# A hybrid of four chunked recurrences on one core: SSD's outputs, gates and norms with channels on partitions, heads on column tiles, norm sums by products

## The chip, the cores and the metric

The kernel runs on one core of a Trainium2 chip. The metric is the device time of one execution, in microseconds; the time before is the median of three runs.

## The reference

One layer of a decoder trunk over 2048 tokens of 1024 channels, float32. The input is normalized (`rmsnorm`) and multiplied by one matrix `w_in`, whose columns feed four mixers of 512 channels each: GLA, mLSTM, HGRN2 and Mamba-2 SSD. Each mixer is a causal recurrence in chunks; its output is normalized in groups, multiplied by a `silu` gate z, and all four go through `w_out`, a residual sum and a last `rmsnorm`. The part that the change is about:

```python
def ssd_chunked(x, a, Bm, Cm, chunk):
    ...
    a_cs = jnp.cumsum(a, axis=-1)
    L = segsum_exp(a)
    CB = jnp.einsum('bclgn,bcsgn->bgcls', Cm, Bm)
    y_diag = jnp.einsum('bgrcls,bcsgrp->bclgrp', CB[:, :, None] * L, x)
    ...
    y_off = jnp.einsum('bclgn,bcgrpn,bgrcl->bclgrp', Cm, states, jnp.exp(a_cs))
    return (y_diag + y_off).reshape(Bsz, S, H, P)

def ssd_branch(...):
    ...
    y = ssd_chunked(xs * dt[..., None], dt * A, Bm, Cm, SSD_CHUNK)
    y = (y + D[:, None] * xs).reshape(Bsz, S, D_BRANCH)
    return grouped_rmsnorm(y * jax.nn.silu(z), norm_w, SSD_GROUPS)
```

SSD has 8 heads of 64 channels in two groups (four heads each share B and C, 128 states), chunks of 128 tokens, and a norm over each group's 256 channels. HGRN2 has 4 heads with 128 keys and 128 values; its scores are `q_i k_j` weighted by a product of decays for each key channel.

## The kernel before, in words

The tokens are cut into two halves of 1024 (`TH`), eight chunks of 128 each. `run` goes through both halves, and in each through the units g0, g1 (GLA), s0, s1 (SSD, four heads each), h0, h1 (HGRN2, two heads each), m0, m1 (mLSTM); then `out_phase` multiplies by `w_out`. A mixer's result goes to the tensor `y` in HBM and is read again in `out_phase`.

The projections split float32 into two parts (high and low, fp32r) and sum three products. `proj_chan` puts 128 output channels on the partitions and 512 tokens on the columns (TensorE tile `ps_c`); `proj_tok2` and `proj_wide` put tokens on the partitions (tile `ps_t`). All other products are plain float32; each stands in the profile as two records of TensorE, as each has two weight loads; a transpose is one record. All of them go through the helper `mm`, line 124, so the profile is read by tiles. The weights come through a ring of nine slots (`load_slot`), issued on the SP queue; in the first half they are split by ScalarE and VectorE and also written to HBM for the second half.

The program is written unit by unit, but a scheduler at build time sets the order on each engine, so a unit's products stand between those of the next unit's projections. Each engine then works through its own list in order. PSUM has four slots for projections (tag `proj`) and four for all else (tag `t`).

In `ssd` (lines 871 to 948) the convolved x, B and C have channels on the partitions (`xc`, `bt`, `ct`). The z gates are projected with tokens on the partitions (`szs`). Then, for each chunk: x and B are transposed (`ps_xt`); the decays `L` of four heads are made from the loaded rows `ab`; `ps_s` holds C·B; the four heads' outputs are four products of 64 columns into `ps_o` (stationary: `L` of a head, moving: x·dt of that head), C·H is one product of 256 columns; `ps_u` is the update of the state `H`. VectorE and GpSimd put the outputs together, multiply by the gate; ScalarE squares with accumulation (`squares`), and at the end of the unit `finish` makes the norm's factors, one for each token, thus one for each partition, scales the rows and writes them through `store` (32x32 transposes on VectorE, four DMAs for each 128 channels and four chunks).

In `lin_steps` HGRN2's scores are built level by level: for block sizes b = 1, 2, 4 to 64 VectorE multiplies the decays of b neighbours into `kb` (line 521) and `qf` (line 522), and TensorE forms the scores between neighbouring blocks. For HGRN2 (`nh == 1`) `mixed` gathers the keys of an even and an odd chunk into one stationary tile of 128 (two ScalarE copies, lines 478 and 479) and makes four products of 128 columns (`ps_s`). The levels 1 to 16 are put into the score tiles by masked copies (lines 499, 545, 546), the levels 32 and 64 by ScalarE copies of the blocks that lie on the diagonal. GLA (`nh == 2`, 64 keys a head) makes its levels 32 and 64 with products of 32 and 64 stationary columns, and its state update (`ps_u<-o_v,t2k`) with two heads beside each other in the partitions of one result.

Of the kernel before, what the change touches and what calls it, by code (L numbers as in the profile page):

```python
# [10 lines left out]
F32 = mybir.dt.float32  # L11
# [4 lines left out]
AF = mybir.ActivationFunctionType  # L16
ALU = mybir.AluOpType
# [4 lines left out]
P = 128  # L22
# [57 lines left out]
def _params(i):  # L80
    cols = []

    def add(key, a):
        PC[key] = sum(c.shape[1] for c in cols)
        cols.append(np.asarray(a, np.float32))

    def rep(v):
        return np.broadcast_to(np.asarray(v).reshape(1, -1), (P, np.asarray(v).size))

    add("nw", i["norm_w"][0].reshape(KT, P).T)  # L90
    add("bw", np.concatenate([i["gla_norm_w"][0], i["ml_norm_w"][0], i["hg_norm_w"][0], i["ssd_norm_w"][0]]).reshape(16, P).T)
# [26 lines left out]
class Kernel:  # L118
# [65 lines left out]

    def row_bcast(self):

        nc = self.nc
# [269 lines left out]
    def lin_steps(self, nh, f, kb, qp, v, sz, car, eps, ycol, vt=None):  # L457
# [58 lines left out]
        while b < C:  # L516
# [18 lines left out]
            if nh == 1:  # L535
# [335 lines left out]
    def ssd(self, q):  # L871
# [12 lines left out]
        w = self.weights(("sz", q))  # L884
        szs = [self.sztile().rearrange("p c (a d) -> p (c a d)", a=1).rearrange("p (c d) -> p c d", c=4) for _ in range(2)]
# [4 lines left out]
        dD = self.dd[:, h4].unsqueeze(2).to_broadcast([P, 4, 64])  # L890
        ss = self.small.tile([P, 16], F32, tag="f_ss", name="f_ss")[:, :8]

        def finish():
            rs = self.rms(ss, 256, 256 * EPS, self.rs2)
            nc.vector.tensor_tensor(rs, rs, self.rs, op=ALU.mult)
            for g in range(2):
                self.scale_rows(szs[g], rs[:, 4 * g:4 * g + 4])
                for j in range(2):
                    self.store(szs[g][:, :, j * P:(j + 1) * P], g, 1536 + 256 * q + j * P)

        for g in range(2):
            yb = szs[g]
            for u in range(2):
                ab = self.up.tile([P, 4, 256], F32, tag="qf", name="ab")
                t0 = g * 512 + u * 256
                nc.sync.dma_start(ab, self.rows[4 + 4 * q:8 + 4 * q, t0:t0 + 256].unsqueeze(0).broadcast_to([P, 4, 256]))
                for j in range(2):
                    c = 2 * u + j
                    cc = 4 * g + c
                    cs = slice(cc * C, (cc + 1) * C)  # L910

                    def hb(t):
                        return t[:, cc, h4].unsqueeze(2).to_broadcast([P, 4, 64])

                    def v4(t):
                        return t.rearrange("p (h d) -> p h d", h=4)

                    pt = self.psp.tile([P, 512], F32, tag="t", name="ps_xt")
                    for i, src in enumerate((xc[0], xc[1], bt)):
                        nc.tensor.transpose(pt[:, i * P:(i + 1) * P], src[:, cs], self.ident)  # L920
                    xx, tb = self.t2k(), self.t2k()
                    xdt, xdd, y1, bk = xx[:, :256], xx[:, 256:], tb[:, :256], tb[:, 256:384]
                    nc.vector.tensor_tensor(v4(xdt), v4(pt[:, :256]), hb(self.dt), op=ALU.mult)
                    nc.vector.tensor_tensor(v4(y1), v4(pt[:, :256]), dD, op=ALU.mult)
                    nc.scalar.copy(bk, pt[:, 256:384])
                    nc.vector.tensor_tensor(v4(xdd), v4(pt[:, :256]), hb(self.dec), op=ALU.mult)
                    ps = self.psp.tile([P, C], F32, tag="t", name="ps_s")
                    self.mm(ps, bt[:, cs], ct[:, cs])
                    L = self.t2k().rearrange("p (h t) -> p h t", h=4)
                    for h in range(4):  # L930
                        nc.vector.scalar_tensor_tensor(out=L[:, h], in0=ab[:, h, j * C:(j + 1) * C], scalar=self.acs[:, cc, 4 * q + h:4 * q + h + 1], in1=self.cmask, op0=ALU.subtract, op1=ALU.min)
                    nc.scalar.activation(L, L, AF.Exp)
                    nc.vector.tensor_tensor(L, L, ps[:, None].to_broadcast([P, 4, C]), op=ALU.mult)
                    po = self.psp.tile([P, 512], F32, tag="t", name="ps_o")
                    for h in range(4):
                        self.mm(po[:, h * 64:(h + 1) * 64], L[:, h], xdt[:, h * 64:(h + 1) * 64])
                    self.mm(po[:, 256:512], ct[:, cs], H)
                    pu = self.psp.tile([P, 256], F32, tag="t", name="ps_u")
                    self.mm(pu, bk, xdd)
                    nc.vector.tensor_tensor(y1, y1, po[:, 0:256], op=ALU.add)  # L940
                    t1 = self.t2k()[:, :256]
                    nc.vector.tensor_tensor(v4(t1), v4(po[:, 256:512]), hb(self.eacs), op=ALU.mult)
                    nc.gpsimd.tensor_tensor(y1, y1, t1, op=ALU.add)
                    nc.gpsimd.tensor_tensor(yb[:, c], y1, yb[:, c], op=ALU.mult)
                    nc.vector.tensor_tensor(v4(H), v4(H), self.el[:, h4, cc:cc + 1].to_broadcast([P, 4, 64]), op=ALU.mult)
                    nc.vector.tensor_tensor(H, H, pu, op=ALU.add)
            self.squares(yb, ss[:, 4 * g:4 * g + 4])
        finish()


    def flat(self, tag, n, dtype=F32):
# [153 lines left out]
    def prepare(self, cp):  # L1105
# [90 lines left out]
```

## Time and profile before

| what | value |
|---|---|
| median of three runs | 2130.73 us (2127.08 to 2130.87) |
| profiled execution: its own time | 2130.25 us |
| its span, first to last instruction | 2128.4 us |
| TensorE busy (matmul) | 2075.1 us, 97% |
| VectorE busy | 1212.8 us, 57% |
| ScalarE busy | 759.0 us, 36% |
| GpSimd busy | 61.0 us, 3% |
| mean granted TensorE clock | 0.993 |

The difference between an execution's own time and its span, 1.85 us, lies around the instructions. A busy time of TensorE is the union of modelled durations of products that overlap in the pipe; the pace of a stream of products is read from how many stand in a stretch of the chain, or from the starts in the timeline. PE is TensorE, DVE VectorE, ACT ScalarE, POOL GpSimd, SP the queue that issues most DMAs.

### The profile page before, as it was taken

What the parts mean: (1) busy time and instruction counts of PE and PEld (TensorE: products, weight loads), DVE (VectorE), ACT (ScalarE), POOL (GpSimd) and SP (SyncE); (2) the same over time, 40 slices, a digit from 0 to 9 for tenths busy, and PEclk for the clock granted to TensorE, in tenths of its full rate; (3) what the DMA queues carried; (4) which work ended last, traced back from release to release, by engine and by line L of the source; (5) the groups of instructions that cost most, each with busy time, mean ns of one, the idle gap of its engine ahead of it and who ended that gap; (6) DMA issues with size and microseconds to landing.
All of it is one profiled execution on the core that took longest, in us unless ns stands there. A gap on an engine that the chain in (4) does not pass through costs nothing.

```text
span 2128.4 us, 31817 instructions
## 1 busy us (share of the span) xinstructions
PE 2075.1 (97%) x12094; PEld 1767.2 (83%) x12094; DVE 1212.8 (57%) x2962; ACT 759.0 (36%) x1889; POOL 61.0 (3%) x96
## 2 busy tenths in 40 slices
PE   7999999999999999999999999999999999999998
PEld 6877898887888888997879887888889898888887
DVE  4465769676565673725466858482826276533332
ACT  5622333435344445324222324342433245212111
POOL 0000001100000000000000201000000000000000
PEclk9999999999999999999999999999999999999999
DMA  8524344535152546342124342322324126422221
GB/s 284 200 90 128 102 139 144 154 91 166 35 189 80 188 117 225 114 160 73 39 98 124 91 118 60 128 55 90 111 89 110 62 103 214 147 89 96 98 74 50
DMA packets 228809, 251.24 MB, mean 118 GB/s; under 512 B 144808, under 2 KB 160280, under 8 KB 228656
## 3 DMA queue, kind: packets, MB, share of 16 engines
q1 hardware_dynamic: 222176, 229.81, 34.3%
q10 hardware_dynamic: 6480, 19.40, 2.6%
q8 instruction: 95, 1.56, 0.3%
q14 instruction: 58, 0.48, 0.1%
HBM read 160.70 MB, written 88.45 MB: 117 GB/s over the span
## 4 chain that ended last, share of the span: by engine, by line
PE 77%; DVE 10%; DMA 6%; ACT 5%; issue 2%; POOL 0%; SPq 0%; DVEq 0%; ACTq 0%; POOLq 0%
PE ps_t L124 24%; PE ps_c L124 21%; PE ps_out L124 15%; PE ps_o L124 5%; PE ps_s L124 5%; DMA raw<-w 2%; PE ps_u L124 2%; PE ps_g L124 2%; DMA ab<-rows 1%; DVE w L223 1%; ACT t2k L637 1%; DVE kc L766 1%; DVE kb L521 1%; DMA t2k<-xT 1%; DMA o_v<-w_out 1%
## 5 line engine op out<-in xcount | busy, mean ns | idle before, releaser
L124 PE MATMUL ps_t<-w,uh 128*128 128x512 f32 (+1 forms) x2560 | 635.7, 339 | 0.5 <-DMA w<-wk 0.5
L124 PE MATMUL ps_c<-uh,w 128*128 128x512 f32 x1792 | 579.8, 400 | 7.2 <-ACT uh L156 7.2
L124 PEld LDWEIGHTS ps_t<-w,uh 128*128 128x128 f32 x2560 | 440.9, 190 | 51.7 <-DMA w<-wk 0.7
L124 PE MATMUL ps_t<-w,ul 128*128 128x256 f32 (+1 forms) x1280 | 432.8, 339 | 0.0
L124 PEld LDWEIGHTS ps_c<-uh,w 128*128 128x128 f32 x1792 | 338.7, 191 | 76.1 <-ACT uh L156 7.6
L124 PE MATMUL ps_c<-ul,w 128*128 128x512 f32 x896 | 357.5, 399 | 0.3 <-DVE ul L157 0.3
L124 PEld LDWEIGHTS ps_t<-w,ul 128*128 128x128 f32 x1280 | 243.7, 190 | 24.1
L124 PEld LDWEIGHTS ps_c<-ul,w 128*128 128x128 f32 x896 | 171.1, 191 | 34.8 <-DVE ul L157 1.1
L223 DVE TENSOR_TENSOR w<-raw,w 128x512 fp32r<-128x512 f32 (+2 forms) x125 | 82.6, 671 | 84.6 <-ACT w L222 83.9
L222 ACT CAST w<-raw 128x512 fp32r<-128x512 f32 (+2 forms) x125 | 74.1, 604 | 82.6 <-DMA raw<-w 51.7
L124 PE MATMUL ps_out<-woh,o_qp 128*128 128x512 f32 x288 | 92.6, 390 | 0.0
L1002 DVE TENSOR_TENSOR o_sz<-o_sz,ps_out 128x512 f32<-128x512 f32 (+1 forms) x33 | 22.0, 670 | 123.6 <-PE ps_out L124 122.3
L124 PE MATMUL ps_out<-woh,o_v 128*128 128x512 f32 (+1 forms) x213 | 75.4, 389 | 0.0
L1003 ACT ACTIVATE ST<-o_sz 128x512 f32<-128x512 f32 (+1 forms) x33 | 20.4, 618 | 123.1 <-DVE o_sz L1002 123.1
L124 PEld LDWEIGHTS ps_out<-woh,o_qp 128*128 128x128 f32 x288 | 54.1, 188 | 11.5
L307 ACT ACTIVATE sz<-ps_t,ss 128x128 f32<-128x128 f32 (+1 forms) x96 | 33.7, 399 | 74.0 <-PE ps_t L124 62.9
L124 PE MATMUL ps_g<-w,uh 128*128 128x288 f32 x256 | 52.9, 302 | 5.9 <-ACT w L222 2.9
L124 PE MATMUL ps_out<-wol,o_qp 128*128 128x512 f32 x144 | 56.2, 391 | 0.3 <-DVE wol L963 0.3
L762 DVE TENSOR_TENSOR craw<-ps_c,rb 128x512 f32<-128x512 f32 x64 | 43.7, 684 | 21.6 <-PE ps_c L124 21.6
L786 ACT ACTIVATE v<-ps_t,ss 128x128 f32<-128x128 f32 x64 | 23.5, 368 | 86.8 <-PE ps_t L124 86.8
L637 ACT ACTIVATE t2k<-ps_o 128x128 f32<-128x128 f32 x128 | 34.6, 286 | 53.6 <-PE ps_o L124 52.6
L521 DVE TENSOR_TENSOR kb<-kb,pl 128x512 f32<-128x512 f32 x72 | 49.9, 693 | 6.3 <-PE ps_s L124 6.3
(355 smaller groups left out, 3357.3 us busy)
## 6 DMA issues: line engine op xcount, KB each, us to landing
wk<-w SPq DMA_DIRECT2D x116, 512.0 KB, 4.4
w<-wk SPq DMA_DIRECT2D x116, 512.0 KB, 5.3
raw<-w SPq DMA_DIRECT2D x115, 256.0 KB, 3.3
y<-t2k SPq DMA_DIRECT2D x256, 64.0 KB, 2.0
t2k<-y SPq DMA_DIRECT2D x64, 256.0 KB, 3.2
t2k<-xT SPq DMA_DIRECT2D x32, 256.0 KB, 4.3
ab<-rows SPq DMA_DIRECT2D x16, 512.0 KB, 5.1
o_sz<-x ACTq DMA_DIRECT2D x16, 512.0 KB, 3.3
```

The lines of the kernel that those rows point to most:

```text
L124: self.nc.tensor.matmul(out, l, r, start=start, stop=stop, skip_group_check=shared)
L222: nc.scalar.copy(t[:, 0, cs], raw[:, cs])
L223: nc.vector.tensor_tensor(t[:, 1, cs], raw[:, cs], t[:, 0, cs].bitcast(F32), op=ALU.subtract)
L307: nc.scalar.activation(out[:, j], ps[:, j], AF.Tanh, scale=self.rsh[:, t + j:t + j + 1])
L521: nc.vector.tensor_tensor(kv[:, :, 0], kv[:, :, 0], pv[:, :, 1:2].to_broadcast([P, n, b]), op=ALU.mult)
L637: self.nc.scalar.activation(junk, ob[:, c], AF.Square, accum_out=ss[:, c:c + 1])
L762: nc.vector.tensor_tensor(rw, ps, self.rb[:, b * 512:(b + 1) * 512], op=ALU.mult)
L766: nc.vector.scalar_tensor_tensor(out=acc, in0=raw[:, k:k + TH], scalar=cw[k], in1=acc, op0=ALU.mult, op1=ALU.add)
L786: nc.scalar.activation(self.mv[i][:, t, :P], ps[:, i * P:(i + 1) * P], AF.Identity, scale=self.rs[:, t:t + 1])
L1002: nc.vector.tensor_tensor(xt[:, ns], xt[:, ns], ps, op=ALU.add)
L1003: nc.scalar.activation(junk[:, ns], xt[:, ns], AF.Square, accum_out=ss[:, i:i + 1])
```

## The change

1. The z gates of SSD are projected with channels on the partitions (`proj_chan`), four results of 512 tokens for each unit and half; the row factors `rb` are multiplied in by VectorE, and the gate is formed by tanh.
2. SSD's outputs are formed with channels on the partitions: for each head one product of the state `H` (64 stationary columns) with `ce` = C·exp(a), and one of x·dt (64 stationary columns) with `L`; two heads lie in partitions 0 to 63 and 64 to 127 of one result. D·x, the sum and the gate take two VectorE instructions for 128 channels and two chunks. GpSimd's part goes away.
3. The norm's sums over 256 channels are products: the squares (ScalarE) stationary, a column of ones moving, one column of result (`ps_q`).
4. The factors go to all partitions by the new function `bcast`, made from `row_bcast`: a transpose, a ScalarE copy, a write to HBM, a broadcast read. Then `zg` is multiplied and written to `y` in one DMA for each 128 channels.
5. HGRN2's levels 32 and 64 are products of 32 and 64 stationary columns, on four and two column tiles; the odd chunks' keys are still taken in reverse (`kr`, one ScalarE copy).

```diff
+    def bcast(self, col, out, tag):
         nc = self.nc
         pt = self.psp.tile([P, 512], F32, tag="t", name="ps_rb")
-        nc.tensor.transpose(pt[:NC, :P], self.rs, self.ident)
+        nc.tensor.transpose(pt[:NC, :P], col, self.ident)
         row = self.t2k()[:NC, :P]
         nc.scalar.copy(row, pt[:NC, :P])
...
+        nc.sync.dma_start(out, rows.broadcast_to([P, TH]))
...
-                ps = mixed(b, qf.rearrange("p (c n two b) -> p c n two b", c=NC, two=2, b=b)[:, :, :, 1])
+                kr = self.t2k()[:, :256].rearrange("p (c n b) -> p c n b", c=NC // 2, b=b)
+                nc.scalar.copy(kr, flipped(C - 1 - b, 2 * b, 64 // b, b))
+                ps = self.psp.tile([P, NC // 2, 2, 64 // b, b], F32, tag="t", name="ps_s")
+                for c in range(NC // 2):
+                    for n in range(64 // b):
+                        for t in range(2):
+                            k0 = (2 * c + t) * C + 2 * n * b
+                            p0 = C - (2 * n + 1) * b if t else 2 * n * b
+                            kk = kr[:, c, 64 // b - 1 - n] if t else kb[:, k0:k0 + b]
+                            self.mm(ps[p0:p0 + b, c, t, n], kk, qf[:, k0 + b:k0 + 2 * b])
...
-        for u, ps in self.proj_tok2(w):
-            self.silu2(szs[u // 2][:, 2 * (u % 2):2 * (u % 2) + 2], ps, 2 * u)
+        for j in range(2):
+            for b in range(2):
+                bs = slice(b * 512, (b + 1) * 512)
+                ps = self.proj_chan(("sz", q), j, b)
+                nc.vector.tensor_tensor(zg[j][:, bs], ps, self.rb[:, bs], op=ALU.mult)
...
-                    for h in range(4):
-                        self.mm(po[:, h * 64:(h + 1) * 64], L[:, h], xdt[:, h * 64:(h + 1) * 64])
-                    self.mm(po[:, 256:512], ct[:, cs], H)
...
+                ce = self.t2k().rearrange("p (h t) -> p h t", h=4)
+                nc.scalar.activation(ce, ab[:, :, js], AF.Exp)
+                nc.vector.tensor_tensor(ce, ce, ct[:, None, cs].to_broadcast([P, 4, C]), op=ALU.mult)
+                for i in range(2):
+                    for l, r, start in ((H, ce, True), (xdt, L, False)):
+                        for h in (2 * i, 2 * i + 1):
+                            o = h % 2 * 64
+                            self.mm(po[o:o + 64, i, j], l[:, h * 64:(h + 1) * 64], r[:, h], start=start, stop=not start)
...
-            self.squares(yb, ss[:, 4 * g:4 * g + 4])
-        finish()
+            for i in range(2):
+                nc.vector.scalar_tensor_tensor(out=xc[i][:, us], in0=xc[i][:, us], scalar=self.dd[:, 2 * q + i:2 * q + i + 1], in1=po[:, i], op0=ALU.mult, op1=ALU.add)
+                nc.vector.tensor_tensor(zg[i][:, us], zg[i][:, us], xc[i][:, us], op=ALU.mult)
+                nc.scalar.activation(sq[:, i], zg[i][:, us], AF.Square)
+            pq = self.psp.tile([P, 2], F32, tag="t", name="ps_q")
+            for j in range(2):
+                for i in range(2):
+                    self.mm(pq[:, j:j + 1], sq[:, i, j * C:(j + 1) * C], self.tri[:, P - 1:P], start=i == 0, stop=i == 1)
+            nc.scalar.copy(ss[:, 2 * u:2 * u + 2], pq)
+        nc.vector.tensor_scalar(out=ss, in0=ss, scalar1=1.0 / 256, scalar2=256 * EPS, op0=ALU.mult, op1=ALU.add)
+        rn = self.flat("v", TH)
+        self.bcast(self.rsqrt(ss, 8), rn, "nsd")
+        for i in range(2):
+            nc.vector.tensor_tensor(zg[i], zg[i], rn, op=ALU.mult)
...
+            nc.sync.dma_start(self.y[t0:t0 + NC, :, :, 12 + 2 * q + i].rearrange("c b r a s -> (b r) c (a s)"), zg[i].rearrange("p (c t) -> p c t", c=NC))
```

The scheduler then sets another order. Three places show it; line numbers are those of the respective kernel.

TensorE in a chunk of s1 in the first half, between the projection products of h0 (`ps_t`); before:

```order
L124 MATMUL ps_t<-w,uh 128x512 x2
L124 MATMUL ps_o<-t2k 128x64 x4
L124 MATMUL ps_o<-hst,ct 128x256
L124 MATMUL ps_u<-t2k 128x256
L920 MATMUL ps_xt<-cf,xc 128x128 x2
L920 MATMUL ps_xt<-cf,v 128x128
L124 MATMUL ps_s<-ct,v 128x128
```

and of the change, an odd chunk of the same unit (`ps_o<-t2k,hst` are the products of H with `ce`, `ps_o<-t2k` those of x·dt with `L`; the last row is the pair's first norm product):

```order
L124 MATMUL ps_o<-t2k,hst 64x128 x2
L124 MATMUL ps_t<-w,uh 128x512 x2
L124 MATMUL ps_o<-t2k 64x128 x2
L124 MATMUL ps_o<-t2k,hst 64x128 x2
L124 MATMUL ps_o<-t2k 64x128 x2
L124 MATMUL ps_t<-w,ul 128x512
L124 MATMUL ps_t<-w,uh 128x512 x2
L124 MATMUL ps_t<-w,ul 128x512
L124 MATMUL ps_t<-w,uh 128x512 x2
L124 MATMUL ps_t<-w,ul 128x512
L124 MATMUL ps_t<-w,uh 128x512 x2
L124 MATMUL ps_q<-cf,t2k 128x1
```

A chunk's output products were one group of five; now they are eight on column tiles, and most chunks have them in two blocks with other products between.

TensorE where s1 ends and the levels of HGRN2's first head begin, first half; before:

```order
L124 MATMUL ps_t<-w,ul 128x512
L124 MATMUL ps_s<-qp,t2k 128x128 x4
L124 MATMUL ps_s<-qp,kb 128x128 x4
L124 MATMUL ps_s<-qp,t2k 128x128 x4
L124 MATMUL ps_t<-w,uh 128x512 x2
L124 MATMUL ps_t<-w,ul 128x512
L124 MATMUL ps_t<-w,uh 128x512 x2
L124 MATMUL ps_s<-qf,t2k 128x128 x4
L124 MATMUL ps_t<-w,ul 128x512
```

and of the change (`ps_rb` is the transpose in `bcast`; the x8 are the levels b = 4 and b = 8):

```order
L124 MATMUL ps_t<-w,ul 128x512
L124 MATMUL ps_q<-cf,t2k 128x1 x4
L194 MATMUL ps_rb<-cf,rs_y 8x128
L124 MATMUL ps_s<-qp,t2k 128x128 x4
L124 MATMUL ps_s<-qp,kb 128x128 x4
L124 MATMUL ps_s<-qp,t2k 128x128 x4
L124 MATMUL ps_s<-qf,t2k 128x128 x8
L124 MATMUL ps_t<-w,uh 128x512 x2
```

The projection products that stood between the levels have moved behind b = 8. In the second half 11 of them stand between the last norm product and the transpose, and 5, 5 and 3 between the transpose and the levels.

VectorE at the same place; before:

```order
L521 TENSOR_TENSOR kb<-kb,pl 128x256x2
L546 COPY_PREDICATED ST_93<-mask,ps_s 128x4x32x2
L545 COPY_PREDICATED ST_93<-mask,ps_s 128x4x64
L521 TENSOR_TENSOR kb<-kb,pl 128x128x4
L546 COPY_PREDICATED ST_93<-mask,ps_s 128x4x32x2
L499 COPY_PREDICATED ST_93<-mask,ps_s 128x4x16x4 x2
L522 TENSOR_TENSOR qf<-qf,pl 128x128x4
```

and of the change, where `o_v` is `rn`, the tile that the broadcast read fills:

```order
L525 TENSOR_TENSOR kb<-kb,pl 128x256x2
L550 COPY_PREDICATED ST_93<-mask,ps_s 128x4x32x2
L549 COPY_PREDICATED ST_93<-mask,ps_s 128x4x64
L317 SCALAR_TENSOR_TENSOR sz<-sz,ps_t 128x128
L550 COPY_PREDICATED ST_93<-mask,ps_s 128x4x32x2
L525 TENSOR_TENSOR kb<-kb,pl 128x128x4
L966 TENSOR_TENSOR sz<-sz,o_v 128x1024 x2
L503 COPY_PREDICATED ST_93<-mask,ps_s 128x4x16x4 x2
L526 TENSOR_TENSOR qf<-qf,pl 128x128x4
```

The two instructions of line 966 have come between the level's `kb` and `qf` steps, and VectorE reaches the second only behind them; the same in the second half.

## Rows read from the trace of the kernel before

**Rows 1.** The page: busy us (share of the span) xinstructions; slices: granted clock in tenths.
```profile
PE 2075.1 (97%) x12094; PEld 1767.2 (83%) x12094; DVE 1212.8 (57%) x2962; ACT 759.0 (36%) x1889; POOL 61.0 (3%) x96
...
PEclk9999999999999999999999999999999999999999
```
**Rows 2.** Windows: the two SSD loops; length, then busy us of PE, PEld, DVE, ACT, POOL.
```profile
285.00:450.00 165.00, 163.61 (x926) 141.58 (x926) 127.98 (x317) 63.84 (x139) 24.65 (x32) 1.00 0.44 134
1160.00:1320.00 160.00, 158.93 (x896) 136.65 (x895) 117.83 (x297) 52.12 (x115) 25.56 (x32) 1.00 0.33 96
```
**Rows 3.** The chain in order of time: start us, us, what.
```profile
1224.56 23.03 PE ps_t L124 x192
...
1637.23 21.79 PE ps_c L124 x96
```
**Rows 4.** Timeline, TensorE in one SSD chunk: start us, us, engine, line, operation.
```profile
391.64 1.08 PE L124 MATMUL ps_o<-t2k 128*128 128x64 f32 x8 [0.35 <-DVE t2k L933]
...
392.55 0.65 PE L124 MATMUL ps_o<-hst,ct 128*128 128x256 f32 x2
...
393.04 0.59 PE L124 MATMUL ps_u<-t2k 128*128 128x256 f32 x2
```
**Rows 5.** Timeline, TensorE in GLA: products on column tiles and their neighbours.
```profile
224.66 1.11 PE L124 MATMUL ps_s<-qf,kb 64*32 64x32 f32 x64
...
228.19 1.15 PE L124 MATMUL ps_s<-qf,kb 64*64 64x64 f32 x32
...
231.54 0.40 PE L124 MATMUL ps_c<-ul,w 128*128 128x512 f32 x1
231.87 1.09 PE L124 MATMUL ps_u<-o_v,t2k 128*64 128x128 f32 x16
232.90 1.27 PE L124 MATMUL ps_o<-o_v,ST 128*128 128x128 f32 x9
```
**Rows 6.** Timeline, TensorE in the levels of HGRN2's first head; in brackets, idle before.
```profile
454.50 1.16 PE L124 MATMUL ps_s<-qp,t2k 128*128 128x128 f32 x8 [0.84 <-ACT t2k L479]
455.50 1.06 PE L124 MATMUL ps_s<-qp,kb 128*128 128x128 f32 x8
456.39 1.14 PE L124 MATMUL ps_s<-qp,t2k 128*128 128x128 f32 x8
...
458.96 1.16 PE L124 MATMUL ps_s<-qf,t2k 128*128 128x128 f32 x8 [0.27 <-ACT t2k L479]
```
**Rows 7.** Timeline of SP in `row_bcast`; the page's issues: count, KB, us to landing.
```profile
55.00 0.51 SPq L193 DMA_DIRECT2D rsd<-t2k  x1
59.59 0.35 SPq L195 DMA_DIRECT2D rb<-rsd  x1
...
rb<-rsd SPq DMA_DIRECT2D x2, 512.0 KB, 3.6
```
**Rows 8.** Groups by line and shape, VectorE: count, busy us, mean ns, idle before.
```profile
L522 DVE TENSOR_TENSOR qf<-qf,pl 128x512 f32<-128x512 f32 x72 | 50.4, 701 | 4.3 <-PE ps_s L124 4.0 <-ACT qp L531 0.2
L499 DVE COPY_PREDICATED ST<-mask,ps_s 128x256 f32<-128x256 uint8 x64 | 29.0, 513 | 5.2 <-PE ps_s L124 4.9
L545 DVE COPY_PREDICATED ST<-mask,ps_s 128x256 f32<-128x256 uint8 x16 | 12.1, 757 | 0.3
L140 DVE SCALAR_TENSOR_TENSOR rs_y<-rs_t,rs_y 128x8 f32<-128x8 f32 x66 | 10.8, 164 | 1.6
L466 DVE TENSOR_TENSOR qf<-qp,f 128x1024 f32<-128x1024 f32 x8 | 10.1, 1262 | 0.5 <-PE ps_o L124 0.3
```
**Rows 9.** A wait of TensorE, and the windows around it (PEclk is third from the end).
```profile
124.16 3.56 PE L124 MATMUL ps_s<-qf,kb 64*128 64x64 f32 x32 [2.23 <-DVE kb L521]
...
117.00:124.00 7.00, 4.93 (x43) 3.48 (x42) 5.26 (x14) 1.27 (x5) 0.00 (x0) 0.96 0.25 86
124.00:131.00 7.00, 6.84 (x40) 6.08 (x41) 3.66 (x7) 0.38 (x1) 0.00 (x0) 0.52 0.30 112
```

More of the change, by code (lines that the diff above doesn't have):

```diff
@@ L185, in row_bcast @@
     def row_bcast(self):
+        self.rb = self.up.tile([P, TH], F32, tag="rb", name="rb")
+        self.bcast(self.rs, self.rb, "rsd")
+    def bcast(self, col, out, tag):
         nc = self.nc
         pt = self.psp.tile([P, 512], F32, tag="t", name="ps_rb")
-        nc.tensor.transpose(pt[:NC, :P], self.rs, self.ident)
+        nc.tensor.transpose(pt[:NC, :P], col, self.ident)
         row = self.t2k()[:NC, :P]
         nc.scalar.copy(row, pt[:NC, :P])
-        rows = self.dram.tile([1, TH], F32, tag="rsd", name="rsd", bufs=2)
+        rows = self.dram.tile([1, TH], F32, tag=tag, name="rsd", bufs=2)
         nc.sync.dma_start(rows.rearrange("o (c t) -> (o c) t", c=NC), row)
-        self.rb = self.up.tile([P, TH], F32, tag="rb", name="rb")
-        nc.sync.dma_start(self.rb, rows.broadcast_to([P, TH]))
+        nc.sync.dma_start(out, rows.broadcast_to([P, TH]))
     def feed(self, n=RING):
@@ L883, in ssd @@
         self.conv_silu2(w, 1, ct, "scw", "scb", 6 + q, 14 + q)
[L884 to L887 removed]
+        zg = [self.sztile().rearrange("p c d -> p (c d)") for _ in range(2)]
+        for j in range(2):
[3 more added lines that the diff above has]
+                nc.vector.tensor_tensor(zg[j][:, bs], ps, self.rb[:, bs], op=ALU.mult)
+                th = self.t2k()
+                nc.scalar.activation(th, zg[j][:, bs], AF.Tanh, scale=0.5)
+                nc.vector.scalar_tensor_tensor(out=zg[j][:, bs], in0=th, scalar=1.0, in1=zg[j][:, bs], op0=ALU.add, op1=ALU.mult)
@@ L901, in ssd @@
[L901 to L929, printed above, removed]
-                    for h in range(4):
[L931 to L935, printed above, removed]
-                        self.mm(po[:, h * 64:(h + 1) * 64], L[:, h], xdt[:, h * 64:(h + 1) * 64])
-                    self.mm(po[:, 256:512], ct[:, cs], H)
[L938 to L946, printed above, removed]
-            self.squares(yb, ss[:, 4 * g:4 * g + 4])
@@ L948, in ssd, with hb, v4 @@
-        finish()
+        for u in range(NC // 2):
+            ab = self.up.tile([P, 4, 256], F32, tag="qf", name="ab")
+            us = slice(u * 256, (u + 1) * 256)
+            nc.sync.dma_start(ab, self.rows[4 + 4 * q:8 + 4 * q, us].unsqueeze(0).broadcast_to([P, 4, 256]))
+            po = self.psp.tile([P, 2, 2, C], F32, tag="t", name="ps_o")
+            for j in range(2):
+                cc = 2 * u + j
+                cs = slice(cc * C, (cc + 1) * C)
+                js = slice(j * C, (j + 1) * C)
+                def hb(t):
+                    return t[:, cc, h4].unsqueeze(2).to_broadcast([P, 4, 64])
+                def v4(t):
+                    return t.rearrange("p (h d) -> p h d", h=4)
+                pt = self.psp.tile([P, 512], F32, tag="t", name="ps_xt")
+                for i, src in enumerate((xc[0], xc[1], bt)):
+                    nc.tensor.transpose(pt[:, i * P:(i + 1) * P], src[:, cs], self.ident)
+                ps = pt[:, 3 * P:]
+                self.mm(ps, bt[:, cs], ct[:, cs])
+                xx, bk = self.t2k(), self.t2k()[:, :P]
+                xdt, xdd = xx[:, :256], xx[:, 256:]
+                nc.vector.tensor_tensor(v4(xdt), v4(pt[:, :256]), hb(self.dt), op=ALU.mult)
+                nc.scalar.copy(bk, pt[:, 256:384])
+                nc.vector.tensor_tensor(v4(xdd), v4(pt[:, :256]), hb(self.dec), op=ALU.mult)
+                L = self.t2k().rearrange("p (h t) -> p h t", h=4)
+                for h in range(4):
+                    nc.vector.scalar_tensor_tensor(out=L[:, h], in0=ab[:, h, js], scalar=self.acs[:, cc, 4 * q + h:4 * q + h + 1], in1=self.cmask, op0=ALU.subtract, op1=ALU.min)
+                nc.scalar.activation(L, L, AF.Exp)
+                nc.vector.tensor_tensor(L, L, ps[:, None].to_broadcast([P, 4, C]), op=ALU.mult)
+                ce = self.t2k().rearrange("p (h t) -> p h t", h=4)
[6 more added lines that the diff above has]
+                            self.mm(po[o:o + 64, i, j], l[:, h * 64:(h + 1) * 64], r[:, h], start=start, stop=not start)
+                pu = self.psp.tile([P, 256], F32, tag="t", name="ps_u")
+                self.mm(pu, bk, xdd)
+                nc.vector.tensor_tensor(v4(H), v4(H), self.el[:, h4, cc:cc + 1].to_broadcast([P, 4, 64]), op=ALU.mult)
+                nc.vector.tensor_tensor(H, H, pu, op=ALU.add)
+            sq = self.t2k().rearrange("p (i t) -> p i t", i=2)
+            for i in range(2):
[3 more added lines that the diff above has]
+            pq = self.psp.tile([P, 2], F32, tag="t", name="ps_q")
+            for j in range(2):
+                for i in range(2):
+                    self.mm(pq[:, j:j + 1], sq[:, i, j * C:(j + 1) * C], self.tri[:, P - 1:P], start=i == 0, stop=i == 1)
+            nc.scalar.copy(ss[:, 2 * u:2 * u + 2], pq)
```

15 lines of the change are left out of this document (4 added, 11 removed).

## Prediction

> **What bounds the kernel now.** I read the page's busy shares first: TensorE is busy for 97% of the span, VectorE for 57% [rows 1], and the granted clock is at its full level in nearly every slice. So a part of the change counts for what it does to TensorE's own work, or for the time that it makes TensorE wait. In the two SSD loops TensorE misses 1.4 us of 165 and 1.1 us of 160 [rows 2]: there is next to nothing to win by relieving VectorE there. The chain in order of time gives the pace of products that follow each other, which mean durations hide, since the products are pipelined: 192 products of 256 columns take 23.03 us and 96 of 512 columns 21.79 us, or 0.227 us each [rows 3]. The timeline of one SSD chunk [rows 4] gives the price of what is replaced there, and two places in GLA already run products on column tiles [rows 5].
>
> **TensorE's work, part by part**
>
> *Z gates.* One `sz` group takes 192 products of 256 columns; with channels on partitions it is 96 of 512. 21.79 - 23.03 = -1.24 us [rows 3], four times: **-5.0 us**. VectorE gets one more pass over 512 columns for each 512 tokens and tile, off the path of an engine that is busy for 57% of the span: nothing.
>
> *SSD outputs.* A chunk now takes 393.04 - 391.64 = 1.40 us for four products of 64 columns and the one of 256 [rows 4]; 32 chunks, 44.8 us. The change makes eight products of 128 columns with 64 stationary columns, alternating between two column tiles. GLA has exactly this: `ps_u` with 128*64, 16 records for eight products [rows 5]. The projection product before it starts at 231.54, so at 231.77 the next could have begun. The block starts 0.10 us late; the full-width products behind it start at 232.90, and nine of them take 1.27 us, where eight take 1.06 and one more would be 0.11 [rows 6]: another 0.10 us lost. The block costs 1.23 us. At half the full-width pace (0.89 us for eight records [rows 6]) the 16 records need 0.90, so entering and leaving the tiles costs 0.33. The order of the change breaks a chunk's eight products into two blocks, mostly 2 and 6: I count 63 blocks. 32 x 0.90 + 63 x 0.33 = 49.6 us: **+4.8 us**.
>
> *Norm sums by products.* Four products of one column for each pair of chunks replace ScalarE's squares with accumulation: 16 pairs x 4 products x 2 records = 128 records. No row has one column. But eight records of 64 columns take 392.55 - 391.64 = 0.91 us [rows 4], as long as eight of 128 [rows 6]: what the columns save is not given back while the stationary side is 128 wide. From above 0.114 us each, 14.6 us; from below the products with 32 stationary columns, 64 records in 1.11 us [rows 5], 2.2 us. I take the upper, whose stationary side is the same: **+14.6 us**. The Trainium skill (TensorEngine Tiling, Instruction Overhead) says that a product of one column costs about 60 cycles, like one of 60; an estimate by that page is 25 ns each, 3.2 us, and the sum would be 11 us lower. No row here decides it; the rows that come nearest speak for the dearer price.
>
> *HGRN2's top levels.* Two groups of eight records, 0.89 us each [rows 6], become 32 records on four tiles and 16 on two. GLA's 64 records of 32 columns take 1.11 us and its 32 of 64 columns 1.15 [rows 5], so 0.28 to 0.56 us and 0.58, each with 0.33 for the switch: 1.52 to 1.80 against 1.78. Eight heads: -2.1 to +0.2 us, I take **-1.0 us**.
>
> Sum of the work: -5.0 + 4.8 + 14.6 - 1.0 = **+13.4 us**.
>
> **The wait that comes new.** Before, the norm's factors lie on the tokens' partitions and are used where they are made. Now they go through `bcast`: transpose, ScalarE copy, a write to HBM and a broadcast read, and only then VectorE multiplies `zg` by `rn` (line 966 of the change). VectorE works in order, and in both halves these two instructions stand ahead of the `qf` step which the fourth group of HGRN2's levels (b = 8) waits for. Counted from the last norm product, at the end of s1: ScalarE's copy and twelve small VectorE instructions of 0.164 us [rows 8], 2.4 us; transpose and copy, 0.6; the write is issued at 55.00 and the read behind it at 59.59, which lands 3.6 us later [rows 7], 8.2 us; two instructions of 1.26 us [rows 8], 2.5; two masked copies of 0.51 and `qf`, 0.70 [rows 8], 1.7. That is 15.4 us. What VectorE does otherwise in that time (six masked copies of 0.51 to 0.76, three `kb` steps of 0.7 [rows 8]) takes 6 us and is over before the read lands. In the first half TensorE has nothing to do in these 15.4 us but the transpose and four groups of eight records, 3.7 us: 11.7 us idle, less the 1.1 us that it waits there today (0.84 + 0.27 [rows 6]): +10.6. In the second half 24 projection products stand between, 24 x 0.227 = 5.4 us: idle 6.3, less 1.1: +5.2. Together **+15.8 us**. The SP queue's weight loads stand behind the same two transfers, but nine slots are loaded ahead; I cost that at nothing, and the ends of the ring are the price if the cover is gone. At the end of s0 the same chain lies beside 71 and 97 projection products (16 and 22 us): nothing.
>
> *Clock.* After a wait of 2.23 us the granted clock was 0.52 for 7 us [rows 9], the lower level (1.2 GHz), after which it came back: half of that time is lost, 3.4 us. The two waits are longer than that one; I take 2.5 us for each, **+5 us**.
>
> *Given back.* The 2.5 us of waits in the SSD loops [rows 2] could go, and ScalarE copies half as much for the two levels: **-2 us**. The 64 transfers with which `store` writes SSD's part of y become eight: off the path.
>
> **Sum.** 13.4 + 15.8 + 5 - 2 = +32.2 us on the profiled execution's 2130.25 us: 2162. That execution lies 0.5 us under the median of the runs, which changes nothing. The ends: work from -0.1 (norm products 2.2, HGRN2 -2.1) to +17 (with a small loss at some 60 more changes of product type), waits and clock from 10 to 40.
>
> **Rivals**
> 1. *The round trip is covered.* If TensorE comes late to s1's end, or the transfers land sooner than 8.2 us, only the work is left: 2130.25 + 13.4 - 2 = 2142. Against it: the chain starts with TensorE's own last product, so its being late moves the whole chain. 15%.
> 2. *VectorE becomes the bound of the SSD loops.* It is busy for 128 of 165 us there [rows 2], and a chunk's results now leave in more, smaller steps (H before each pair of products, `ce`, two gate steps for two chunks). One more microsecond in each of 32 chunks gives 2194, half of that 2178. For it: VectorE's share; against: per pair of chunks it loses as many passes over 256 columns as it gets. 12%.
> 3. *Faster: stationary data is in place ahead of each switch.* If a block on column tiles costs its 0.90 us alone and a norm product 0.017, the work is -5.0 - 16.0 + 2.2 - 7.4 = -26.2; with the waits and the rest (+18.8) the sum is -7.4: 2123. It ends as soon as a block loses more than 0.09 us at its edges (79 blocks); GLA's lost 0.33. 6%.
> 4. *The tiles do not run at the same time*, so that the change does not do what it says: 16 records of 0.112 for a chunk, +28 us over the sum: 2190. GLA's blocks speak plainly against it. 4%.
>
> **How the numbers follow.** My forecast, 60%, is 2162, for itself 2148 to 2178. What is left, 3%, lies within 0.2% of the time before (4.3 us, about what a measurement of this kernel can tell from no change), where cheap norm products meet a covered chain. The range takes in rival 1 and most of 2: 2139 to 2188. Faster 6%, same 4% (with the edge of rival 1), slower 90%.
>
> **What would show it.** In the changed profile: eight products of 128*64 at some 0.056 us a record with gaps of 0.1 us at both edges; norm products at 0.11 us a record and 14 us in all; TensorE waiting at one place in each half, where s1's last chunk ends and h0's levels begin, where VectorE's line 966 is released by the transfer `o_v<-rsd`, and the lower clock behind it. Wrong would make it: norm products at 0.03 us, line 966 without a wait, or `ps_s` after it not idle.

## The result and the profile after

| what | before | after |
|---|---|---|
| median of four runs | 2130.80 us (2127.08 to 2132.52) | 2165.69 us (2161.02 to 2166.82) |
| profiled execution: its span | 2128.4 us | 2163.1 us |
| mean granted TensorE clock | 0.993 | 0.986 |

The ratio is 1.016, with a 95% interval of 1.0141 to 1.018: the change costs 34.9 us. The forecast was 2162. The total came out; the path to it was right in the work and wrong in what TensorE waits for.

The changed kernel's page, first part and TensorE's clock, which answer to [rows 1]:

```profile
PE 2097.8 (97%) x12290; PEld 1744.1 (81%) x12290; DVE 1224.0 (57%) x2930; ACT 768.2 (36%) x1877; POOL 10.9 (1%) x32
...
PEclk9999999989999999999999999999999999999999
```

TensorE has 22.7 us more busy time, part of it at the lower clock. VectorE and ScalarE have hardly more, and GpSimd's busy time falls from 61.0 to 10.9 us. The two SSD loops, in windows of the changed kernel ([rows 2] before):

```profile
285.00:450.00 165.00, 160.81 (x901) 123.75 (x899) 125.63 (x279) 63.65 (x118) 0.00 (x0) 0.97 0.41 129
1160.00:1320.00 160.00, 159.86 (x899) 124.93 (x897) 114.94 (x247) 53.91 (x97) 0.00 (x0) 1.00 0.36 113
```

In the second half nothing is lost: 0.14 us of 160. In the first half TensorE misses 4.2 us of 165, and the granted clock is 0.97, where it was 1.00. VectorE is less busy there than before, so it did not become the bound of these loops (rival 2).

What TensorE waits for in the changed kernel, the rows that bear on the change (engine, tile, what it waits for, us in total, times, longest):

```profile
PE ps_s L124 <- DVE qf L526: 8.4, 5, 4.2
...
PE ps_q L124 <- ACT t2k L956: 4.0, 3, 1.7
...
PE ps_rb L194 <- DVE rs_y L140: 2.8, 1, 2.8
...
PE ps_s L124 <- ACT t2k L483: 2.1, 4, 1.0
```

Before, `qf` was 0.4 us, the next two did not exist, and the last was 3.1 us. The granted clock of five stretches around and behind these waits (us, busy time of PE, PEld, DVE, ACT, POOL; then the granted clock):

```profile
322.00:326.00 4.00, 4.00 (x14) 2.66 (x13) 3.87 (x9) 1.23 (x3) 0.00 (x0) 0.57 0.76 225
356.00:363.00 7.00, 7.00 (x21) 5.70 (x21) 3.73 (x16) 1.09 (x3) 0.00 (x0) 0.54 0.76 248
452.00:459.00 7.00, 5.38 (x25) 5.10 (x25) 3.54 (x9) 3.07 (x10) 0.00 (x0) 0.51 0.20 75
462.00:469.00 7.00, 3.78 (x13) 3.43 (x14) 6.85 (x17) 2.86 (x10) 0.00 (x0) 0.52 0.53 159
1350.00:1357.00 7.00, 6.37 (x23) 5.63 (x24) 4.03 (x11) 2.77 (x9) 0.00 (x0) 0.53 0.41 120
```

All five lie at the lower level (1.2 GHz) for most of their time. Two are in s0's loop of the first half, which the prediction did not have; three are where s1 ends and h0 begins.

**The place where s1 ends, first half.** The timeline of the changed kernel (start, us, engine, line, operation; in brackets the idle time before it and what ended it):

```profile
448.99 0.83 PE L124 MATMUL ps_q<-cf,t2k 128*128 128x1 f32 x6 [0.94 <-ACT t2k L956]
...
450.05 0.17 DVE L962 TENSOR_SCALAR f_ss<-f_ss 128x8 f32<-128x8 f32 x1 [1.56 <-ACT f_ss L961]
...
452.58 0.37 PE L194 MATMUL ps_rb<-cf,rs_y 128*8 128x128 f32 x1 [2.76 <-DVE rs_y L140]
453.04 0.26 ACT L196 COPY t2k<-ps_rb 8x128 f32<-8x128 f32 x1 [3.03 <-PE ps_rb L194]
453.20 0.41 ACT L482 COPY t2k<-kb 128x256 f32<-128x256 f32 x1
453.32 0.29 SPq L198 DMA_DIRECT2D rsd<-t2k  x1
...
453.99 2.08 PE L124 MATMUL ps_s<-qp,t2k 128*128 128x128 f32 x8 [1.04 <-ACT t2k L483]
454.61 0.32 SPq L199 DMA_DIRECT2D o_v<-rsd  x1
...
459.86 1.16 PE L124 MATMUL ps_s<-qf,t2k 128*128 128x128 f32 x8 [0.58 <-ACT t2k L483]
...
461.46 2.35 DVE L966 TENSOR_TENSOR sz<-sz,o_v 128x1024 f32<-128x1024 f32 x2
...
465.22 1.20 PE L124 MATMUL ps_s<-qf,t2k 128*128 128x128 f32 x4 [4.20 <-DVE qf L526]
```

The chain behind the last norm product stands, on three engines at once, ahead of HGRN2's first level in lists that are worked off in order: on VectorE its twelve small steps ahead of `kb`, on TensorE its transpose ahead of the levels' products, on ScalarE its copy (line 196) ahead of the level's copies (482 and 483), though these need nothing of it. In TensorE's list nothing else stands there: h0's projection products, which lay between the levels before, come only behind the group of 465.22. TensorE idles 0.94 us for the last squares, then 2.76, 1.04 and 0.58, runs the first levels at half clock (2.08 us for eight records, against 1.16 in [rows 6]), and waits 4.20 us more, while VectorE works without a pause (7.00 us of 7 from 459 to 466) on masked copies, `kb` steps and line 966. Line 966, however, has no bracket: it did not wait for the read. For all four units the trace has this of it:

```profile
L966 DVE TENSOR_TENSOR sz<-sz,o_v x8: 1215/1220/1229, 370.5 to 1348.0; 128x1024 f32<-128x1024 f32 x8
its engine sat idle before it (us, times) until:
  DMA o_v<-rsd: 0.5, 1
```

So the trip through HBM cost 0.5 us of one engine's waiting, at an end of s0; at the two ends of s1, where TensorE waits, it cost none. The prediction had taken it for the cause.

**The wait in s0's loop, first half**, timeline of the changed kernel:

```profile
354.57 0.62 ACT L226 CAST w<-raw 128x512 fp32r<-128x512 f32 x1 [5.50 <-DMA raw<-w]
355.10 0.41 ACT L956 ACTIVATE t2k<-sz 128x256 f32<-128x256 f32 x1
...
355.56 0.38 PE L124 MATMUL ps_q<-cf,t2k 128*128 128x1 f32 x2 [1.67 <-ACT t2k L956]
355.80 0.71 PE L124 MATMUL ps_c<-uh,w 128*128 128x512 f32 x2
```

The squares (line 956) stand in ScalarE's list behind the cast of a weight slot, which waits 5.50 us for its weights. Before, nobody waited for the squares until the unit's end; now a product does, so TensorE waits for a weight transfer through ScalarE. The other wait of this kind, 1.40 us, has the same cast ahead of it, with 2.78 us for its weights. Only the first half casts weights, and only it shows these waits. The last two rows also give a norm product's price: two records in 0.24 us, 0.12 each.

### The profile page after: what moved, and what is told of

It reads as the page before. It is cut to its first block, busy times and chain, and to the rows that moved or that the text cites. A ratio compares the mean times of both kernels' runs of the same rounds, so it can differ in the third digit from the quotient of the medians.

```text
span 2163.1 us, 31843 instructions
## 1 busy us (share of the span) xinstructions
PE 2097.8 (97%) x12290; PEld 1744.1 (81%) x12290; DVE 1224.0 (57%) x2930; ACT 768.2 (36%) x1877; POOL 10.9 (1%) x32
## 4 chain that ended last, share of the span: by engine, by line
PE 79%; DVE 9%; DMA 5%; ACT 5%; issue 1%; SPq 0%; ACTq 0%; DVEq 0%
PE ps_c L124 27%; PE ps_t L124 21%; PE ps_out L124 15%; PE ps_o L124 5%; PE ps_s L124 4%; PE ps_u L124 3%; DMA raw<-w 2%; PE ps_g L124 2%; DMA w<-wk 1%; DVE w L227 1%; DVE kc L779 1%; DVE kb L525 1%; ACT t2k L650 1%; ACT w L226 1%; PE ps_xt L927 1%
## 5 line engine op out<-in xcount | busy, mean ns | idle before, releaser
L124 PE MATMUL ps_c<-uh,w 128*128 128x512 f32 x2048 | 671.8, 403 | 7.7 <-ACT uh L156 7.7
L124 PE MATMUL ps_t<-w,uh 128*128 128x512 f32 (+1 forms) x2048 | 545.8, 354 | 1.1 <-DMA w<-wk 1.1
L124 PEld LDWEIGHTS ps_c<-uh,w 128*128 128x128 f32 x2048 | 388.0, 191 | 88.9 <-ACT uh L156 8.1
L124 PE MATMUL ps_c<-ul,w 128*128 128x512 f32 x1024 | 411.9, 402 | 0.3 <-DVE ul L157 0.3
L124 PEld LDWEIGHTS ps_t<-w,uh 128*128 128x128 f32 x2048 | 360.2, 190 | 53.3 <-DMA w<-wk 1.9
L124 PE MATMUL ps_t<-w,ul 128*128 128x512 f32 (+1 forms) x1024 | 360.8, 353 | 0.0
L124 PEld LDWEIGHTS ps_c<-ul,w 128*128 128x128 f32 x1024 | 196.1, 191 | 40.7 <-issue 1.5
L124 PEld LDWEIGHTS ps_t<-w,ul 128*128 128x128 f32 x1024 | 194.2, 190 | 25.2 <-issue 0.7
L317 DVE SCALAR_TENSOR_TENSOR sz<-sz,ps_t 128x128 f32<-128x128 f32 x64 | 17.5, 286 | 70.8 <-ACT sz L316 45.6
L124 PEld LDWEIGHTS ps_s<-qf,kb 64*128 64x128 f32 (+4 forms) x960 | 38.4, 148 | 22.0 <-issue 18.4
```

Of the source, the lines that this page charges most:

```text
L124: self.nc.tensor.matmul(out, l, r, start=start, stop=stop, skip_group_check=shared)
L317: nc.vector.scalar_tensor_tensor(out=out, in0=out, scalar=1.0, in1=ps, op0=ALU.add, op1=ALU.mult)
```

## The experiments

Each number has its own runs of the kernel before beside it. "The order" means that a chunk's products with `L` stand before those with `H`; "the chain" is what follows s1's last norm product up to line 966.

**1. HGRN2's levels alone**, on the kernel before:

```diff
-                ps = mixed(b, qf.rearrange("p (c n two b) -> p c n two b", c=NC, two=2, b=b)[:, :, :, 1])
+                kr = self.t2k()[:, :256].rearrange("p (c n b) -> p c n b", c=NC // 2, b=b)
...
+                            self.mm(ps[p0:p0 + b, c, t, n], kk, qf[:, k0 + b:k0 + 2 * b])
```

> The kernel before, with HGRN2's levels 32 and 64 on column tiles and nothing else of the change. Theory (work on TensorE decides): two groups of 0.89 us become 0.27 + 0.33 and 0.58 + 0.33 us for each of eight heads, -0.3 us each: 2.4 us faster than before, 2128. Rival (switching between tile shapes is the change's loss, here as well): 16 more switches, 5 us slower, 2136.

Measured 2129.6 us (ratio 0.999, 0.9978 to 1.0001). A small gain or none, as the term said; the levels do not cost.

**2. The order.** 32 blocks on column tiles instead of 63:

```diff
-                    for l, r, start in ((H, ce, True), (xdt, L, False)):
+                    for l, r, start in ((xdt, L, True), (H, ce, False)):
```

> The changed kernel with the two products of a head in the other order: x*dt with L first, H with ce behind it. The same products and the same sums; a chunk's eight products then stand in one block on column tiles (32 blocks instead of 63). Theory (each block loses 0.33 us at its edges): 31 x 0.33 = 10 us faster than the change, 2155. Rival (the edges cost nothing, the loss is norm products and waits): within 2 us of 2166.

Measured 2168.99 us (1.0178, 1.016 to 1.0196): nothing gained. Its page and its waits:

```profile
PE 2088.3 (97%) x12290; PEld 1747.9 (81%) x12290; DVE 1226.0 (57%) x2930; ACT 767.3 (35%) x1877; POOL 10.9 (1%) x32
```

```profile
PE ps_s L124 <- DVE qf L526: 9.1, 5, 4.2
...
PE ps_q L124 <- ACT t2k L956: 5.9, 4, 2.2
PE ps_rb L194 <- DVE rs_y L140: 5.5, 2, 2.8
PE ps_s L124 <- ACT t2k L483: 4.1, 5, 1.0
```

TensorE's busy time did fall, by 9.5 us, close to 31 blocks x 0.33 = 10.2. Most of it came back in these four waits: 24.6 us against 17.3 in the changed kernel. TensorE came earlier to places that others set.

**3. Line 966 later.** s1's multiply and the write of y stand behind h0's `hvz` projections, the rest of the chain stays:

```diff
+                if p == 0:
+                    self.late()
...
+        self.late = late
+        if q == 0:
+            late()
```

> The changed kernel with s1's last multiplication by the norm factors (line 966) and its write of y moved in the program behind the projection loop of h0. TensorE's list stays nearly as it is, VectorE has the two instructions behind the levels' steps. Theory (TensorE waits there for VectorE, which waits for the broadcast read): the waits of 4.2 and 3.7 us and two stretches at the lower clock go, 12 to 15 us faster than the change, 2152. Rival (only TensorE's longer work counts, and the time comes back elsewhere): within 3 us of 2166.

Measured 2160.93 us (1.0137, 1.0118 to 1.0155), nearer to the rival. Its waits:

```profile
PE ps_s L124 <- DVE qf L526: 3.9, 5, 1.9
...
PE ps_rb L194 <- DVE rs_y L140: 2.8, 1, 2.8
```

The wait for `qf` falls by 2.3 us in each half (4.2 to 1.9 and 3.5 to 1.2): by what the two multiplies themselves take on VectorE, 2.35 us. The other waits at the place stay. This is where the prediction's mechanism began to fall: if the read were the cause, moving its only reader would have freed more than the reader's own time.

**4. The norm products twice** (the second set's result is not read):

```diff
-            pq = self.psp.tile([P, 2], F32, tag="t", name="ps_q")
-            for j in range(2):
+            pq = self.psp.tile([P, 4], F32, tag="t", name="ps_q")
+            for j in (2, 3, 0, 1):
...
```

> The changed kernel with every norm product made twice, the second into columns that nobody reads. Theory (a product of one column costs what its 128 stationary columns cost, 0.11 us a record): 128 x 0.11 = 14 us slower than the change, 2180. Rival (it costs what one moving column costs, 0.025 us): 3 us slower, 2169.

Measured 2180.77 us (1.0225, 1.0204 to 1.0246): 15.1 us more than the changed kernel for 128 records, 0.118 us each; the spread of the runs leaves several us of doubt, too few to reach the 3 us of the rival. The column count of one gives nothing back.

**5. No chain at all.** The norm's factors are left out; line 966 multiplies by rows that are there already:

```diff
-        rn = self.flat("v", TH)
-        self.bcast(self.rsqrt(ss, 8), rn, "nsd")
         for i in range(2):
-            nc.vector.tensor_tensor(zg[i], zg[i], rn, op=ALU.mult)
+            nc.vector.tensor_tensor(zg[i], zg[i], self.rb, op=ALU.mult)
```

> The changed kernel, but line 966 multiplies by the rows rb that are there already; the norm's factors, their transpose and the trip through HBM are left out (the norm products and their copies stay). Theory (the new wait is the trip's): the two waits for qf go from 8.4 us to about 1, the wait of 2.8 us for rs_y goes, and with them three stretches of lower clock behind them, 10 us in all: some 2147. Rival (the late multiply gained only 5 us: the levels wait for VectorE's own steps because no projection products stand between them, and the trip only lies beside that): 2159.

Measured 2139.47 us (1.0045, 1.003 to 1.006), below both, with a mean granted clock of 0.992. Its wait for `qf`:

```profile
PE ps_s L124 <- DVE qf L526: 0.7, 3, 0.2
```

The chain with all that follows from it costs 2165.69 - 2139.47 = 26.2 us; everything else that the change does costs 2139.47 - 2130.08 = 9.4. What follows from it takes in the order: here the scheduler puts projection products between h0's levels again, and the waits for the squares fall from 4.0 to 1.1 us.

**6. Norm sums by an all-ones matrix.** The sums appear on every partition, so the chain is gone without leaving anything out:

```diff
+            pq = self.psp.tile([P, 256], F32, tag="t", name="ps_q")
+            for i in range(2):
+                self.mm(pq, self.ones, sq[:, i], start=i == 0, stop=i == 1)
+            nc.scalar.copy(rn[:, u * 256:(u + 1) * 256], pq)
...
+            nc.scalar.activation(rn, rn, AF.Ln, scale=1.0 / 256, bias=self.eps)
+            nc.scalar.activation(rn, rn, AF.Exp, scale=-0.5)
```

> The changed kernel with the norm sums made by an all-ones stationary matrix of 128 x 128 (fp32r; the squares of two chunks, 2 products of 256 columns a pair), one pair later than the squares, so that every partition has the sum and no transpose, no HBM write and no broadcast read is needed; the factors by ScalarE's Ln and Exp; for s1 the multiply stands behind h0's hvz projection. Theory (the norm products' 128 records of 0.11 us and the trip are what makes the change slow): work -12 us, waits and clock -15 us: about 2139. Rival (the wait stays, since the levels lack products between them): 2152.

Measured 2131.41 us (1.0005, 0.9991 to 1.002): level with the kernel before, and 34.3 us under the changed one. This run changes several things at once (fp32r products, made a pair later than the squares, the chain gone, s1's multiply late), so the gain is that of all of them.

**7. The same with the order:**

> As the all-ones kernel, and a chunk's products in the order L before H, so that there are 32 blocks on column tiles instead of 63. Theory (half the blocks, 8.9 us less work as with the order alone, and the places where that came back as waits, the norm products' squares and the trip, are gone): 2130, level with the kernel before. Rival (the 8.9 us come back as waits for VectorE again, since H's update now stands before its product): as the all-ones kernel without it, about 2139.

Measured 2125.38 us (0.9973, 0.9963 to 0.9983): faster than the kernel before, by 0.3%, and than the changed one. The order, worth nothing in the changed kernel, is worth 6 us here. Its place where s1 ends, first half:

```profile
437.94 0.28 PE L124 MATMUL ps_q<-t2k,ones 128*128 128x256 f32 x1
438.06 0.39 PE L124 MATMUL ps_t<-w,uh 128*128 128x512 f32 x1
...
438.88 0.36 PE L124 MATMUL ps_q<-t2k,ones 128*128 128x256 f32 x1
439.08 0.83 PE L124 MATMUL ps_s<-qp,t2k 128*128 128x128 f32 x6
...
448.30 1.13 PE L124 MATMUL ps_s<-qf,t2k 128*128 128x128 f32 x8 [1.10 <-DVE qf L526]
```

From start to start the last pair's two norm products take 0.12 and 0.20 us, and the levels do not wait for them.

**8. The gate's multiply on GpSimd**, on top of 7:

```diff
-                nc.vector.tensor_tensor(zg[i][:, us], zg[i][:, us], xc[i][:, us], op=ALU.mult)
+                nc.gpsimd.tensor_tensor(zg[i][:, us], zg[i][:, us], xc[i][:, us], op=ALU.mult)
```

> As the all-ones kernel with L before H, and the multiply by the gate (two of 128 x 256 for a pair of chunks, 64 in all of some 0.4 us) on GpSimd instead of VectorE. Theory (what is still lost in the first half's SSD loops is TensorE waiting for VectorE, 3.4 us for the scores of L): VectorE's busy time falls by some 27 us, the waits for L by 2 to 3 us: about 2122.5. Rival (GpSimd takes longer for the same pass and the norm's squares come late, or VectorE's order and not its load makes the waits): 2125 or more.

Measured 2126.34 us (0.9977, 0.9963 to 0.9991): no difference from 7. I had miscounted: it is 32 instructions, not 64, so some 13 us of VectorE. The waits for the scores of `L` did fall, from 3.4 to 1.8 us, but a wait for the squares, 0.9 us, came instead. The multiply in 7 and in 8:

```profile
L967 DVE TENSOR_TENSOR sz<-sz,xc 128x256 f32<-128x256 f32 x32 | 13.4, 419 | 0.0
...
L967 POOL TENSOR_TENSOR sz<-sz,xc 128x256 f32<-128x256 f32 x32 | 25.0, 789 | 355.6 <-DVE xc L966 321.0 <-DMA ab<-rows 34.4
```

VectorE's busy time fell only from 1214.0 to 1209.2 us. Rows of its other instructions add up to some 3 us more; the rest of the difference is not explained.

**9. The chain late.** Nothing left out and the trip kept, but s1's whole chain stands behind h0's `hvz` projections:

```diff
+            if (p, j) == (0, 0):
+                self.late()()
...
+        def late():
+            nc.vector.tensor_scalar(out=ss, in0=ss, scalar1=1.0 / 256, scalar2=256 * EPS, op0=ALU.mult, op1=ALU.add)
+            rn = self.flat("v", TH)
+            self.bcast(self.rsqrt(ss, 8), rn, "nsd")
...
```

> The changed kernel, but s1's whole chain behind its last norm product (the twelve small VectorE steps, the transpose, ScalarE's copy, write, broadcast read and the multiply) stands behind h0's hvz projections instead of ahead of h0's levels; nothing is left out and the trip through HBM stays. Theory (what costs is the place of the chain's steps in the in-order lists of TensorE, ScalarE and VectorE, ahead of the levels, not the transfers): the waits for rs_y (2.8 us), t2k and qf (8.4 us) go and the lower clock behind them, some 18 us of the 26 that leaving the chain out gave: about 2146. Rival (the transfers cost: TensorE or VectorE then waits for them at the new place, as the late multiply alone, which gained 5 us): 2160.

Measured 2149.9 us (1.0094, 1.0077 to 1.0112): 15.8 us gained (14 by the ratios) where moving line 966 alone gained 4.8. TensorE's waits for `rs_y` and `qf` have no row over 1 us any more, and projection products stand between h0's levels again:

```profile
457.32 1.16 PE L124 MATMUL ps_s<-qf,t2k 128*128 128x128 f32 x8 [0.26 <-ACT t2k L483]
458.23 0.48 PE L124 MATMUL ps_t<-w,ul 128*128 128x512 f32 x1
```

So the gain is that of the chain's place together with the order that the scheduler sets by it; no run separates the two. Line 966, here line 972, now does wait for the trip, and through VectorE's list TensorE waits too, for line 624 behind it:

```profile
499.76 2.36 DVE L972 TENSOR_TENSOR sz<-sz,o_v 128x1024 f32<-128x1024 f32 x2 [1.72 <-DMA o_v<-rsd]
...
502.03 1.49 DVE L624 SCALAR_TENSOR_TENSOR st<-st,pl,ps_u 128x128 f32<-128x128 f32 x4
...
502.43 0.49 PE L124 MATMUL ps_o<-st,qf 128*128 128x128 f32 x2 [1.82 <-DVE st L624]
```

So in the changed kernel it is the chain's place that cost, not its transfers; at the new place the transfers cost 1.8 us. The profiled executions of this kernel and of 5 are 8.7 us apart. This wait is 1.8 of them, and the waits for the squares, 3.0 us against 1.1, another 1.9; part of the rest is the lower clock behind the longest of these (0.72 from 360 to 370; in 5 it is 0.69 from 325 to 330), and what remains is not explained.

**10. The chain late, with the order:**

> As the late chain, and a chunk's products in the order L before H. Theory (the waits in which the order's 8.9 us were lost are those of the chain): about 2138, half the blocks on column tiles now pay. Rival (they are lost at the norm products, which wait for ScalarE's squares in s0's loop): 2145.

Measured 2141.66 us (1.0062, 1.0039 to 1.0085), between the two. Its runs lie in two groups, three from 2135.5 to 2138.3 and three from 2145.0 to 2148.1, and the trace is one of the first group. By the medians the order pays here, some 7 to 8 us, though the intervals of 9 and 10 still touch: with the chain out of the way, the work that it saves is not taken back, though one wait for the squares, 2.2 us, is left in the trace.

## Why the prediction was right, and where it was not

- **The sum.** Work less what was given back was 13.4 - 2 = 11.4; without the chain the change costs 9.4 (run 5). Wait and clock were 15.8 + 5 = 20.8; the chain cost 26.2. Together 35.6 against 32.2: errors of opposite sign, so that the total fits as well as it does is luck.
- **Norm products, +14.6: right.** Run 4 gives 15.1. The estimate that I worked out from the Trainium skill (TensorEngine Tiling (Array Packing), Instruction Overhead), 25 ns each, is off by a factor of nearly five here: the measurement, 0.118 us, decides. It is about the pace of products of 64 and 128 columns with 128 stationary columns (0.114 in [rows 4], 0.111 in [rows 6]). Rival 3 rested on cheap products and fell with it.
- **SSD outputs, +4.8: the price of a block holds.** Run 2 takes 31 blocks away and TensorE's busy time falls by 9.5 us, 0.31 each against the 0.33 forecast. The timeline of a chunk in the changed kernel:

```profile
391.83 0.27 PE L927 MATMUL ps_xt<-cf,xc 128*128 128x128 f32 x1
392.04 0.44 PE L124 MATMUL ps_o<-t2k 128*64 128x128 f32 x4
392.31 0.39 PE L124 MATMUL ps_o<-t2k,hst 128*64 128x128 f32 x4
392.52 0.39 PE L124 MATMUL ps_o<-t2k 128*64 128x128 f32 x4
392.84 0.33 PE L927 MATMUL ps_xt<-cf,xc 128*128 128x128 f32 x1
```

  Four records in 0.21 us inside a block, 0.053 each, so the tiles do run at the same time (rival 4); 0.1 us is lost ahead of the block and 0.1 behind it.
- **HGRN2, -1.0: right** as far as run 1 can tell. **Z gates, -5.0**: not measured alone. Terms and measurements leave the work 2 us under the sum.
- **The step that failed: that "VectorE's line 966 is released by the transfer `o_v<-rsd`".** Right were the engines and the two places: where s1 ends TensorE waits 9.5 us in the first half and 3.8 in the second, 2.6 of which it had before at these places, so 10.7 new against 15.8 forecast. The rows of the second half, and the row of the kernel before at the same place:

```profile
PE ps_s L124 <- DVE qf L526: 3.5, 1, 3.5
PE ps_s L124 <- ACT t2k L483: 0.3, 1, 0.3
...
PE ps_s L124 <- ACT t2k L479: 1.5, 2, 1.2
```

  But the read was issued 1.3 us behind the write, not the 4.6 of [rows 7], and line 966 found its data there: it stood without a wait, one of the signs that the prediction had named for being wrong. The twelve small steps, the transpose and the copies, in the prediction only the first 3.0 us of line 966's path, were what everybody stood behind: I summed their time as a path for line 966, and did not ask what else was queued behind each of them. The forecast that TensorE would wait at one place in each half, for VectorE behind line 966, was therefore wrong; in the first half it waits before five groups of records where s1 ends. From the last norm product's end to the group that waits for `qf` there pass 15.4 us (449.82 to 465.22), just the length forecast, and this too is luck: the 8.2 us for write and read are not in it, but the levels' products at the lower clock and VectorE's own work.
- **The waits for the squares, 4.0 us (0.9 of them counted above), were not in the prediction.** "VectorE gets one more pass" and its like priced each engine's load, and ScalarE's load is small; its list holds casts that wait up to 5.5 us for weights, and a product now hangs on it.
- **Clock, +5: too small.** The prediction had two stretches; there are five. Span times the missing share of the clock is 2128.4 x 0.007 = 14.9 us before and 2163.1 x 0.014 = 30.3 after; a part of these 15 us lies in time in which TensorE waited anyway. It is the term that made good for the waits that came out smaller.
- **Rival 1** (the round trip is covered) was true of the transfers in the changed kernel and yet not of the time.

## What to carry to other kernels

A new chain of tiny steps between two stages is priced by what stands behind each of its steps in every engine's list, not by its own length: ask of each copy, transpose and scalar step which independent work of the next stage it delays, and place the chain behind that work; where a scheduler sets the order, look at what it then leaves between the next stage's products. When a result that was needed at a unit's end becomes an operand of TensorE, look at what else its producer's list waits for, transfers above all. A reduction over partitions whose result is wanted on all partitions cost less here as a product with an all-ones stationary matrix (2 products of 256 columns for a pair of chunks, their multiply placed late) than as one-column products and a broadcast. A saving in TensorE's work shows in the time only once the waits behind it are gone.

## What the runs showed of the hardware

- A float32 product with one moving column takes 0.118 us a record (run 4; 0.12 in the timeline), like one of 64 columns (0.114, [rows 4]) or of 128 (0.111, [rows 6]) with the same 128 stationary columns.
- A wait of 1.67 us was followed by a granted clock of 0.54 over 7 us (356 to 363), so by the lower of the two levels; [rows 9] had it after 2.23 us. Around the wait of 4.20 us it was 0.52 (462 to 469), behind the second half's wait of 3.5 us 0.53 (1350 to 1357): the short wait was dearer for its length than the long ones. Not every short wait was followed by it: behind one of 1.12 us in run 5 the granted clock was 0.69 (325 to 330), behind one of 1.21 us in run 9 it was 1.00 (315 to 345).
- A multiply of 128 x 256 took 0.42 us on VectorE and 0.79 on GpSimd (runs 7 and 8); 32 of them taken off VectorE lowered its busy time by 4.8 of some 13 us.
